# Bisection steps queued behind regular work, and duration estimates from measurements, in a hybrid encoder step

## The chip, the cores and the metric

The kernel runs on 1 core of one Trainium2 chip. The metric is device time in microseconds (us), the median of several runs: 1571.07 us before the change (3 runs, 1570.73 to 1572.39).

## The reference, cut to what matters

One layer of a streaming encoder runs on a prompt of 1024 frames (eight tiles of 128 rows) and on 8 samples of 16 new frames each with 512 cached keys (a ninth tile, called tile 8). Two mixers work side by side, a linear recurrence and a sparse attention, then a SwiGLU block. Everything is in float32.

```python
proj = rmsnorm(x, norm_mix) @ w_in                  # xr, gate, q, k, v, qi, ki, wi
xc = causal_conv(xr, conv_prev, conv_w, conv_b)     # 4 taps
r, i = sigmoid(xc @ w_rg + b_rg), sigmoid(xc @ w_ig + b_ig)     # 8 blocks of 64
h_t = a_t * h_(t-1) + sqrt(1 - a_t^2) * i_t * xc_t  # a = exp(-8 r softplus(-lambda))
y_a = h * gelu(gate)
idx = sum_h relu(qi_h . ki) * wi_h                  # indexer score per query and key
sel = top_k(where(chunk-causal, idx, -inf), 256)    # 132 for the samples
y_b = softmax(q . k[sel] / 8) @ v[sel]
x = x + concat(y_a, y_b) @ w_out
x = x + (silu(g) * u) @ w_ffn_out                   # g, u = rmsnorm(x) @ w_ffn_in
```

The top-k keeps for each query row the keys whose index score is among its best. The kernel doesn't sort: it finds each row's threshold by bisection and turns the scores into an additive mask.

## The kernel before, in words

Matrix products are done in float32 split into a high and a low part, so one product is three matmuls. The stages follow each other on TensorE: norm and key/value projection (to about 70 us), index scores (to 183), the recurrence, called LRU (to 355), query projection (to 433), first half of the output projection, called out-A, with rope of the keys (to 505), attention (to about 700), second half of the output projection, and the feed-forward block to the end.

**The bisection.** Tiles 2 to 8 need a threshold. Two groups are formed (TK): tiles 2 to 5 on ScalarE, where a count is a pass of Sign with an accumulator, and tiles 6, 7 and 8 on VectorE. VectorE's group copies the upper halves of the scores into 16-bit keys, does 16 rounds, makes new keys of the lower halves (topk_lower), does 16 more rounds, computes a threshold (topk_threshold) and turns each tile into a mask (topk_mask). A round is one count for each of the three tiles (tensor_scalar with accum_out, out to the scratch jk), and two to four operations on 128x3 numbers that set the next candidate. The masks of tile 6, 7 and 8 end in two GpSimd operations each. Attention on a tile waits for its mask; the samples wait for the masks of tile 7 and 8, because two constants of theirs are cast into the buffers of the keys and of the scratch.

**What sets the order.** Each stage is a set of Python generators, and run() steps them along a clock of its own. TensorE's time is added in mm(), that of the other engines in Metered.call, which raises busy[engine] by an estimate for each instruction. A generator yields how long its next step isn't due. The two bisections are "side" generators, tied to an engine by the table filler. Such a step is taken in run() when the clock has come to the engine's busy time less SLACKS[phase], and in fill() when a regular instruction leaves a gap of at least FILL = 1.0 us on its engine. All steps go through step(). The order in which instructions are handed out gives their priority; a scheduler behind it then orders each engine's queue by its own model of readiness and by priority. Before, step() lowers a bisection step's priority by 400 (LATER) and leaves the place to that scheduler.

On the chip each engine runs its queue in the order written; an instruction whose input isn't there holds what stands behind it.

Of the kernel before, what the change touches and what calls it, by code (L numbers as in the profile page):

```python
# [11 lines left out]
BF16 = mybir.dt.bfloat16  # L12
I32 = mybir.dt.int32
I16 = mybir.dt.int16
# [21 lines left out]
class Metered:  # L36


    def __init__(self, engine, kernel, name, fixed, each):
        self.engine, self.kernel, self.name, self.fixed, self.each = engine, kernel, name, fixed, each  # L40

    def __getattr__(self, op):
        f = getattr(self.engine, op)
        if op in ("dma_start", "wait", "semaphore") or not callable(f):
            return f

        def call(*args, **kw):
            n = 1
            for a in args:
                if hasattr(a, "shape") and len(a.shape) > 1:  # L50
                    n = max(n, int(np.prod(a.shape[1:])))
            each = self.each
            if self.name == "vector" and op in ("tensor_copy", "tensor_scalar") and "accum_out" not in kw:
                each *= 0.5
            if self.name == "vector" and kw.get("accum_out") is not None and args[1].dtype in (BF16, I16):
                each *= 0.5
            k = self.kernel
            start = k.now() if k.chain is None else k.chain + k.HOP
            k.fill(self.name, start)
            end = max(k.busy[self.name], start) + self.fixed + n * each  # L60
            if self.name == "scalar" and op == "activation":
                end += k.table(args[2])
            k.busy[self.name] = end
            if k.chain is not None:
                k.chain = end
            return f(*args, **kw)  # L66

        return call


class Engines:
    def __init__(self, nc, kernel):
        self.nc = nc
        for name, fixed, each in (("vector", 0.07, 0.00104), ("scalar", 0.2, 0.00072), ("gpsimd", 0.05, 0.0012)):
            kernel.busy[name] = 0.0
            setattr(self, name, Metered(getattr(nc, name), kernel, name, fixed, each))

    def __getattr__(self, x):
        return getattr(self.nc, x)
# [2 lines left out]
class Kernel:  # L82
    def __init__(self, ctx, tc, I, O):
        self.ctx, self.tc, self.I, self.O = ctx, tc, I, O
        self.pe = self.pe0 = 0.0
        self.clock = 0.0
        self.phase = 0
        self.chain = None
        self.busy, self.filler, self.side, self.gap = {}, {}, [], None
        self.nc = Engines(tc.nc, self)  # L90


    def run(self, streams, width, side=(), carry=()):
# [7 lines left out]
        def due(x):  # L101
            e = self.filler.get(x[1])
            return x[0] if e is None else max(x[0], self.busy[e] - self.SLACKS[self.phase])

# [49 lines left out]

    def step(self, g):

        n = self.LATER.get(self.filler.get(g), 0)
        if not n:
            return next(g, None)
        with self.tc.high_priority(offset=-n):  # L160
            return next(g, None)

    def begin(self):

# [27 lines left out]
    TABLES = {"exp": (AF.Exp, AF.Tanh), "sqrt": (AF.Sqrt,), "gelu": (AF.Gelu_apprx_tanh, AF.Tanh), "silu": (AF.Silu,)}  # L192
    SYNC = 0.3
    HOP = 0.1
    SLACKS = (1.5, 1.5, -3.0, -3.0, 1.5)
    QUEUE = 8.0
    AHEAD = 2.0

# [1 line left out]
    def mm(self, out, lhsT, rhs, start, stop):  # L200
        n = 1
        for v in rhs.shape[1:]:
            n *= v
        self.pe += max(n, 256 if lhsT.shape[-1] > 64 else 128) / 2400.0
        self.nc.tensor.matmul(out, lhsT, rhs, start=start, stop=stop)  # L205

    def mm4(self, out, lhsT, rhs, start, stop):
# [1538 lines left out]
```

## Time and profile before

| | before |
|---|---|
| median of 3 runs | 1571.07 us |
| the profiled execution | 1569.72 us |
| its span, first to last instruction | 1567.9 us |
| TensorE busy | 1446.7 us (92%) |
| VectorE busy | 916.7 us (58%) |
| ScalarE busy | 626.2 us (40%) |
| GpSimd busy | 312.8 us (20%) |
| mean granted TensorE clock | 0.96 |

The profile cuts the span into 40 slices and gives each engine's busy share in tenths, and it follows the chain of work that ended last. VectorE stands at 9 tenths or more from the sixth to the thirteenth slice and between 1 and 4 in most of the later half, while TensorE stands at 9 from the fourteenth slice on, the last excepted. Shares over the whole span therefore hide which engine sets the pace where. PE is TensorE, PEld its weight loads, DVE VectorE, ACT ScalarE, POOL GpSimd and SP the queue that issues transfers.

### The profile page before, as it was taken

The numbers are of one execution on the slowest core, as the hardware profiler recorded it, in microseconds if no ns is written. First come the engines' busy times: TensorE is split into PE (matmuls) and PEld (weight loads), VectorE is DVE, ScalarE is ACT, GpSimd is POOL, SyncE is SP. The second block draws the span as 40 slices with busy tenths as digits, with TensorE's granted clock in tenths as the row PEclk, the third lists the DMA queues.
The fourth block names the chain that finished last, engine by engine and source line by source line (L and its number), as shares of the span: only waits on it lengthen the run. The fifth ranks groups of instructions, "written<-read, shape, count | busy, mean of one in ns | idle before, by whom it ended". The sixth has DMA issues, their size and how long they took to land.

```text
span 1567.9 us, 20857 instructions
## 1 busy us (share of the span) xinstructions
PE 1446.7 (92%) x7754; PEld 1322.8 (84%) x7754; DVE 916.7 (58%) x1957; ACT 626.2 (40%) x1481; POOL 312.8 (20%) x453
## 2 busy tenths in 40 slices
PE   6889887756888999999999999999999999999998
PEld 6777777746766788888999999999898989898987
DVE  7556899999999888768324233333324242424143
ACT  6457968875633978655302020202120212111110
POOL 4215225541986434400000000000000000000000
PEclk8999898877898999999999999999999999999999
DMA  7201101100320002121202020202020201111003
GB/s 239 56 16 42 35 16 29 29 27 14 134 71 22 1 14 57 39 68 42 81 13 81 1 81 0 81 0 81 1 81 15 67 28 54 41 41 54 28 1 121
DMA packets 93797, 74.65 MB, mean 48 GB/s; under 512 B 13236, under 2 KB 84532, under 8 KB 93696
## 3 DMA queue, kind: packets, MB, share of 16 engines
q1 hardware_dynamic: 93696, 73.32, 15.5%
q8 instruction: 61, 1.00, 0.3%
q14 instruction: 40, 0.33, 0.1%
HBM read 67.03 MB, written 6.27 MB: 47 GB/s over the span
## 4 chain that ended last, share of the span: by engine, by line
PE 72%; DVE 18%; ACT 4%; issue 3%; DMA 1%; POOL 1%; SPq 0%; POOLq 0%; ACTq 0%; DVEq 0%
PE ps L205 67%; DVE jk L66 7%; PE ps L215 4%; DVE tk_cand L66 2%; DVE tr L66 1%; DVE xc L66 1%; ACT jk L66 1%; DVE qn L66 1%; DVE ti L66 1%; PE ps L210 1%; DVE tk_cnt L66 1%; DVE s L66 1%; DVE kn L66 0%; ACT relu L66 0%; DVE acc L66 0%
## 5 line engine op out<-in xcount | busy, mean ns | idle before, releaser
L205 PE MATMUL ps<-hf,w 128*128 128x384 f32 x2556 | 460.6, 338 | 0.0
L205 PEld LDWEIGHTS ps<-hf,w 128*128 128x128 f32 x2556 | 451.5, 187 | 0.8
L205 PE MATMUL ps<-w,a 128*128 128x512 f32 x999 | 239.1, 390 | 0.0
L66 DVE TENSOR_TENSOR acc<-ps,acc 128x512 f32<-128x512 f32 x234 | 161.3, 690 | 119.7 <-PE ps L205 119.2
L205 PEld LDWEIGHTS ps<-w,a 128*128 128x128 f32 x999 | 187.3, 188 | 40.1
L66 DVE TENSOR_TENSOR sg<-ps,sg 128x384 f32<-128x384 f32 x66 | 36.8, 557 | 281.7 <-PE ps L205 281.1
L66 ACT ACTIVATE w<-raw 128x512 fp32r<-128x512 f32 x128 | 77.7, 629 | 300.9 <-PE ps L205 220.0
L66 DVE TENSOR_TENSOR w<-raw,w 128x512 fp32r<-128x512 f32 x116 | 76.8, 688 | 85.0 <-ACT w L66 84.9
L66 ACT ACTIVATE a<-sg 128x384 fp32r<-128x384 f32 x66 | 34.5, 523 | 222.1 <-DVE sg L66 222.1
L66 ACT ACTIVATE jk<-s,tk_cand 128x384 bf16<-128x384 f32 (+3 forms) x128 | 99.8, 779 | 40.7 <-DVE tk_cand L66 36.8
L205 PE MATMUL ps<-hf,rest 128*128 128x384 f32 x612 | 114.5, 334 | 0.0
L205 PE MATMUL ps<-w,h 128*128 128x256 f32 (+1 forms) x600 | 102.6, 332 | 11.6 <-ACT sq L66 7.8
L205 PE MATMUL ps<-h,w 128*128 128x384 f32 x576 | 108.5, 348 | 0.5 <-ACT relu L66 0.5
L205 PEld LDWEIGHTS ps<-h,w 128*128 128x128 f32 x576 | 106.6, 198 | 0.6 <-ACT relu L66 0.6
L205 PEld LDWEIGHTS ps<-hf,rest 128*128 128x128 f32 x612 | 106.9, 188 | 0.2
L205 PEld LDWEIGHTS ps<-w,h 128*128 128x128 f32 x600 | 90.1, 207 | 18.3 <-ACT sq L66 8.2
L205 PE MATMUL ps<-w,rest 128*128 128x512 f32 x324 | 83.2, 406 | 11.3 <-POOL rest L66 11.1
L205 PEld LDWEIGHTS ps<-w,rest 128*128 128x128 f32 x324 | 61.0, 193 | 26.3 <-POOL rest L66 12.7
L66 ACT ACTIVATE sg<-ps 128x384 f32<-128x384 f32 x66 | 32.0, 485 | 121.3 <-PE ps L205 121.3
L205 PE MATMUL ps<-xh,bd 128*128 128x384 f32 x72 | 22.0, 426 | 46.3 <-ACT xh L66 40.6
L66 POOL TENSOR_SCALAR m<-m,mx 128x128 f32<-128x128 f32 (+7 forms) x64 | 47.5, 748 | 67.4 <-DVE mx L66 60.3
L205 PEld LDWEIGHTS ps<-xh,bd 128*128 128x128 f32 x72 | 15.1, 234 | 51.0 <-ACT xh L66 43.0
(263 smaller groups left out, 2221.0 us busy)
## 6 DMA issues: line engine op xcount, KB each, us to landing
raw<-in_w_ffn_in_dram SPq DMA_DIRECT2D x44, 512.0 KB, 3.9
raw<-in_w_ffn_out_dram SPq DMA_DIRECT2D x22, 512.0 KB, 3.6
raw<-in_w_in_dram SPq DMA_DIRECT2D x16, 512.0 KB, 5.1
out_dram<-acc SPq DMA_DIRECT2D x9, 512.0 KB, 2.6
x<-in_x_prompt_dram SPq DMA_DIRECT2D x8, 512.0 KB
acc<-in_x_prompt_dram SPq DMA_DIRECT2D x8, 512.0 KB, 4.2
tab<-in_rope_dram SPq DMA_DIRECT2D x34, 64.0 KB, 1.9
raw<-in_w_out_dram SPq DMA_DIRECT2D x4, 512.0 KB, 3.5
```

Of the source, the lines that this page charges most:

```text
L66: return f(*args, **kw)
L205: self.nc.tensor.matmul(out, lhsT, rhs, start=start, stop=stop)
L210: self.nc.tensor.matmul(out, lhsT, rhs, start=start, stop=stop)
L215: self.nc.tensor.transpose(out, in_, self.ident[0:n, 0:n])
```

## The change

Three things are changed. The estimates of VectorE, ScalarE and GpSimd are computed by a new function cost() with a fixed part and a part per element for each kind of operation; that of a matmul becomes its columns at 2.4 GHz plus 0.0167 us in place of at least 256 (or 128) columns. SLACKS becomes 0.5 in each phase. And each regular instruction of the three engines is recorded with its estimated end, so that step() can look up the last one on the step's engine whose end isn't later than the clock and give the step's instructions an edge to it: on that engine they may not stand ahead of it.

```diff
@@ -36,8 +36,8 @@
 class Metered:
 
 
-    def __init__(self, engine, kernel, name, fixed, each):
-        self.engine, self.kernel, self.name, self.fixed, self.each = engine, kernel, name, fixed, each
+    def __init__(self, engine, kernel, name):
+        self.engine, self.kernel, self.name = engine, kernel, name
 
     def __getattr__(self, op):
         f = getattr(self.engine, op)
@@ -45,35 +45,47 @@
             return f
 
         def call(*args, **kw):
-            n = 1
-            for a in args:
-                if hasattr(a, "shape") and len(a.shape) > 1:
-                    n = max(n, int(np.prod(a.shape[1:])))
-            each = self.each
-            if self.name == "vector" and op in ("tensor_copy", "tensor_scalar") and "accum_out" not in kw:
-                each *= 0.5
-            if self.name == "vector" and kw.get("accum_out") is not None and args[1].dtype in (BF16, I16):
-                each *= 0.5
             k = self.kernel
             start = k.now() if k.chain is None else k.chain + k.HOP
             k.fill(self.name, start)
-            end = max(k.busy[self.name], start) + self.fixed + n * each
+            end = max(k.busy[self.name], start) + self.cost(op, args, kw)
             if self.name == "scalar" and op == "activation":
                 end += k.table(args[2])
             k.busy[self.name] = end
             if k.chain is not None:
                 k.chain = end
-            return f(*args, **kw)
+            said = f(*args, **kw)
+            if not k.filling:
+                k.issued[self.name].append((end, said.ins))
+            return said
 
         return call
+
+    def cost(self, op, args, kw):
+        tensors = [a for a in args if hasattr(a, "shape") and len(a.shape) > 1]
+        n = max([1] + [int(np.prod(a.shape[1:])) for a in tensors])
+        wide = [a for a in tensors if int(np.prod(a.shape[1:])) == n]
+        here = all(a.space == bass.MemoryType.SB for a in wide)
+        accum = kw.get("accum_out") is not None or op == "tensor_tensor_reduce"
+        one = op in ("tensor_copy", "tensor_scalar", "memset")
+        if self.name == "scalar":
+            return 0.2 + n * 0.0008 + 0.19 * accum
+        if self.name == "gpsimd":
+            return 0.1 + n * 0.0011 if one else 0.2 + n * 0.0023
+        if op == "tensor_tensor_scan":
+            return 0.2 + n * 0.0022
+        if one and not accum:
+            return 0.1 + n * (0.00026 if here and all(a.dtype in (BF16, I16) for a in wide) else 0.00052 if here else 0.00104)
+        return 0.157 + n * 0.00104 + 0.08 * accum + 0.1 * (here and not one)
 
 
 class Engines:
     def __init__(self, nc, kernel):
         self.nc = nc
-        for name, fixed, each in (("vector", 0.07, 0.00104), ("scalar", 0.2, 0.00072), ("gpsimd", 0.05, 0.0012)):
+        for name in ("vector", "scalar", "gpsimd"):
             kernel.busy[name] = 0.0
-            setattr(self, name, Metered(getattr(nc, name), kernel, name, fixed, each))
+            kernel.issued[name] = []
+            setattr(self, name, Metered(getattr(nc, name), kernel, name))
 
     def __getattr__(self, x):
         return getattr(self.nc, x)
@@ -87,6 +99,7 @@
         self.phase = 0
         self.chain = None
         self.busy, self.filler, self.side, self.gap = {}, {}, [], None
+        self.issued, self.filling = {}, False
         self.nc = Engines(tc.nc, self)
 
 
@@ -154,11 +167,20 @@
 
     def step(self, g):
 
-        n = self.LATER.get(self.filler.get(g), 0)
-        if not n:
+
+        e = self.filler.get(g)
+        if e is None:
             return next(g, None)
-        with self.tc.high_priority(offset=-n):
-            return next(g, None)
+        now = self.clock if self.gap is None else self.gap
+        last = next((i for t, i in reversed(self.issued[e]) if t <= now), None)
+        with ExitStack() as st:
+            st.enter_context(self.tc.high_priority(offset=-self.LATER[e]))
+            if last is not None:
+                st.enter_context(self.tc.issue_after(last))
+            self.filling = True
+            lat = next(g, None)
+            self.filling = False
+        return lat
 
     def begin(self):
 
@@ -192,7 +214,7 @@
     TABLES = {"exp": (AF.Exp, AF.Tanh), "sqrt": (AF.Sqrt,), "gelu": (AF.Gelu_apprx_tanh, AF.Tanh), "silu": (AF.Silu,)}
     SYNC = 0.3
     HOP = 0.1
-    SLACKS = (1.5, 1.5, -3.0, -3.0, 1.5)
+    SLACKS = (0.5, 0.5, 0.5, 0.5, 0.5)
     QUEUE = 8.0
     AHEAD = 2.0
 
@@ -201,7 +223,7 @@
         n = 1
         for v in rhs.shape[1:]:
             n *= v
-        self.pe += max(n, 256 if lhsT.shape[-1] > 64 else 128) / 2400.0
+        self.pe += n / 2400.0 + 0.0167
         self.nc.tensor.matmul(out, lhsT, rhs, start=start, stop=stop)
 
     def mm4(self, out, lhsT, rhs, start, stop):
```

All instructions are the same ones and the same number of each; the last 4310 of TensorE's 7724 instructions stand in the same order. Three places where the order differs are shown. s_892, s_893 and s_894 are the scores of tiles 6, 7 and 8, s_889 to s_891 those of tiles 3 to 5; jk_911 is the scratch of VectorE's bisection, jk_912 of ScalarE's; sp_p, sp_e, prm and hb are small parameters of the recurrence, xc its convolution.

VectorE at the start of its bisection, before: the last index scores of tile 7 are followed by this.

```order
L66 SCALAR_TENSOR_TENSOR s_893<-relu,wi,s_893 128x512 x3
L66 MEMSET s_893 64x64
L66 COPY prm<-ps 128x160
L66 MEMSET sp_p 128x4
L66 COPY key<-s_893 128x1024
L66 TENSOR_SCALAR hb<-prm 128x8
L66 TENSOR_SCALAR sp_e<-prm 128x4
L66 TENSOR_SCALAR jk_911,tk_cnt<-key,tk_cand 128x1024
L66 TENSOR_TENSOR sp_e<-sp_e,prm 128x4
L66 TENSOR_SCALAR jk_911,tk_cnt<-key,tk_cand 128x528
```

Seven more counts stand between these rows and the first row of the convolution; some ten rows earlier tile 6's keys had been copied and counted, among tile 7's scores.

The same place in the changed order, up to the convolution.

```order
L57 TENSOR_TENSOR sp_p<-sp_p,sp_z 128x4
L57 TENSOR_SCALAR sp_p<-sp_p 128x4
L57 TENSOR_TENSOR sp_p<-sp_p,sp_s 128x4
L57 SCALAR_TENSOR_TENSOR sp_p<-sp_p,sp_e 128x4
L57 TENSOR_SCALAR sp_2069<-sp_p 128x4
L57 TENSOR_SCALAR m_2070<-sp_p 128x4
L57 TENSOR_SCALAR jk_911,tk_cnt<-key,tk_cand 128x896
L57 TENSOR_SCALAR jk_911,tk_cnt<-key,tk_cand 128x1024
L57 SCALAR_TENSOR_TENSOR xc<-xp,prm,xc 128x384
L57 TENSOR_SCALAR jk_911,tk_cnt<-key,tk_cand 128x528
L57 SCALAR_TENSOR_TENSOR xc<-xp,prm,xc 128x384
```

The three key copies stand ahead of these rows, among the steps of sp_p, and behind all index scores; two counts in place of ten stand ahead of the first convolution row.

VectorE at the end of its bisection, before: in out-A, among the rope of queries and keys, the last of tile 8.

```order
L66 TENSOR_TENSOR tail<-tail 128x72
L66 TENSOR_TENSOR qn<-qn,tab 128x256
L66 TENSOR_TENSOR kn<-kn,rp 128x128
L66 TENSOR_SCALAR jk_912,tk_cnt<-s_890,tk_cnt 128x640
L66 TENSOR_TENSOR acc<-ps,acc 128x512
L66 TENSOR_TENSOR qn<-qn,rp 128x256
L66 TENSOR_SCALAR tail<-tail 128x72
L66 TENSOR_TENSOR qn<-qn,rp 128x256
L66 CAST jk_911<-s_894 128x528
L66 TENSOR_SCALAR jk_912,tk_cnt<-s_891,tk_cnt 128x768
```

The cast of tile 8's finished scores stands long before attention begins.

The end of the bisection in the changed order: in attention; m<-ps,s_892 (named ISA) takes the masked scores of tile 6, and smr and rest are the split probabilities of tiles before it.

```order
L57 SCALAR_TENSOR_TENSOR key<-jk_911 128x896
L57 TENSOR_SCALAR s_892,tk_cnt<-s_892,tk_cnt 128x896
L57 TENSOR_TENSOR smr<-ps,smr 128x512
L57 TENSOR_SCALAR tk_cnt<-tk_cnt 128x1
L57 SCALAR_TENSOR_TENSOR jk_911<-key,tk_cnt,jk_911 128x896
L57 TENSOR_TENSOR smr<-ps,smr 128x512 x2
L57 TENSOR_SCALAR jk_911<-s_893,tk_cnt 128x1024
L57 SCALAR_TENSOR_TENSOR key<-jk_911 128x1024
L57 TENSOR_SCALAR s_893,tk_cnt<-s_893,tk_cnt 128x1024
L57 ISA m,mx<-ps,s_892 128x448
```

Ahead of attention's first row stood 96 counts and all masks before; now 72 counts stand there, and 24 counts and the masks of tiles 6, 7 and 8 come in attention.

TensorE at the first sample's scores (ps<-jk_911,key), before.

```order
L205 MATMUL ps<-k_4345,qeo 128x384
L205 MATMUL ps<-k_4346,qeo 128x384
L205 MATMUL ps<-k_4345,qeo 128x384
L205 MATMUL ps<-k_4346,qeo 128x384
L205 LDWEIGHTS key
L205 MATMUL ps<-jk_911,key 128x264
L205 MATMUL ps<-smr,rest 128x264
L215 MATMUL ps<-ident,m 128x128 x2
L205 LDWEIGHTS key
L205 MATMUL ps<-jk_911,key 128x264
```

They stand among the products of tile 5 (128x384), ahead of tile 6.

The same place in the changed order.

```order
L227 MATMUL ps<-k_4254,qeo 128x448
L227 MATMUL ps<-k_4253,qeo 128x448
L237 MATMUL ps<-ident,m 128x128
L227 MATMUL ps<-smr,vhl 128x512 x3
L237 MATMUL ps<-ident,m 128x128 x8
L227 MATMUL ps<-smr,vhl 128x512 x8
L227 LDWEIGHTS key
L227 MATMUL ps<-jk_911,key 128x264
L227 MATMUL ps<-rest 128x264 x3
L227 LDWEIGHTS key
```

They stand behind tile 6's first eight score products (128x448) and the last probability products of tile 5.

## Rows read from the trace of the kernel before

**Rows 1.** Five windows; columns: stretch, length, busy us per engine, granted clock, DMA share, GB/s.
```profile
core 0: us, PE busy (x) PEld busy (x) DVE busy (x) ACT busy (x) POOL busy (x), PEclk, DMA share, GB/s
0.00:174.00 174.00, 146.43 (x749) 123.38 (x749) 114.50 (x239) 104.77 (x262) 63.01 (x120) 0.92 0.29 84
174.00:200.00 26.00, 25.52 (x135) 23.33 (x135) 22.61 (x59) 25.29 (x54) 3.77 (x6) 1.00 0.09 23
200.00:507.00 307.00, 227.87 (x1233) 209.78 (x1232) 301.75 (x684) 189.78 (x519) 176.20 (x233) 0.86 0.14 44
507.00:585.00 78.00, 72.60 (x412) 61.43 (x412) 68.72 (x235) 66.44 (x162) 32.13 (x50) 0.94 0.03 8
585.00:1567.90 982.90, 974.24 (x5231) 904.92 (x5229) 409.09 (x746) 239.89 (x487) 37.67 (x44) 1.00 0.15 46
```

**Rows 2.** Groups of TensorE, 174 to 507 us: busy, mean ns, idle before, releaser.
```profile
L205 PE MATMUL ps<-xh,bd 128*128 128x384 f32 x72 | 22.0, 426 | 46.3 <-ACT xh L66 40.6 <-POOL xh L66 4.5 <-POOL xp L66 1.1
L205 PE MATMUL ps<-w,h 128*128 128x256 f32 x432 | 59.9, 305 | 11.6 <-ACT sq L66 7.8 <-DVE to L66 3.8
L205 PE MATMUL ps<-w,rest 128*128 128x512 f32 x108 | 31.1, 428 | 11.1 <-POOL rest L66 11.1
```

**Rows 3.** Groups of VectorE by shape, 200 to 507 us: counts of the bisection.
```profile
L66 DVE TENSOR_SCALAR_CACHE_REDUCE jk<-key,tk_cnt 128x1024 bf16<-128x1024 int16 x16 | 20.4, 1273 | 0.2
L66 DVE TENSOR_SCALAR_CACHE_REDUCE jk<-key,tk_cnt 128x896 bf16<-128x896 int16 x16 | 18.3, 1142 | 0.2
L66 DVE TENSOR_SCALAR_CACHE_REDUCE jk<-key,tk_cnt 128x528 bf16<-128x528 int16 x16 | 12.1, 756 | 0.2
L66 DVE DVE_READ_ACCUMULATOR jk<-key,tk_cnt 128x1 f32 x48 | 3.9, 81 | 0.0
L66 DVE TENSOR_SCALAR tk_cand<-tk_cnt 128x3 f32<-128x3 f32 x16 | 4.1, 258 | 0.2
L66 DVE SCALAR_TENSOR_TENSOR tk_cnt<-tk_cand,tk_cnt 128x3 f32<-128x3 f32 x16 | 4.1, 256 | 0.2
```

**Rows 4.** Timeline of VectorE, 410 to 460 us: mask of tile 7, and a cast.
```profile
426.22 0.94 DVE L66 TENSOR_SCALAR jk<-s,tk_cnt 128x1024 bf16<-128x1024 f32 x1
427.20 3.27 DVE L66 TENSOR_TENSOR_SCAN key<-jk 128x1024 int16<-128x1024 bf16 x1
430.39 1.25 DVE L66 TENSOR_SCALAR_CACHE_REDUCE s<-s,tk_cnt 128x1024 f32<-128x1024 f32 x1
433.13 1.27 DVE L66 SCALAR_TENSOR_TENSOR jk<-key,tk_cnt,jk 128x1024 bf16<-128x1024 int16 x1
435.40 2.64 DVE L66 CAST key<-ident 128x1024 bf16<-128x1024 f32 x1
```

**Rows 5.** Timeline of GpSimd, 440 to 460 us: last two mask steps of tile 8.
```profile
449.36 1.19 POOL L66 TENSOR_TENSOR s<-s,jk 128x528 f32<-128x528 f32 x1
451.96 0.84 POOL L66 TENSOR_SCALAR s<-s 128x528 f32<-128x528 f32 x1
```

**Rows 6.** Groups of VectorE by shape, 507 to 700 us: attention.
```profile
L66 DVE CUSTOM_DVE_ANT_0 m<-ps,s 128x448 f32<-128x448 f32 x8 | 5.0, 620 | 0.2
L66 DVE TENSOR_TENSOR smr<-ps,smr 128x512 fp32r<-128x512 f32 x60 | 40.6, 686 | 6.4 <-ACT smr L66 5.9
```

**Rows 7.** Timeline of TensorE, 570 to 592 us: first sample score, first product of tile 6.
```profile
575.34 0.27 PE L205 MATMUL ps<-jk,key 128*128 128x264 bf16 x1
583.20 0.98 PE L205 MATMUL ps<-k,qeo 128*128 128x448 f32 x4
```

**Rows 8.** Timeline of TensorE, VectorE and ScalarE around 205 us, a row or two each.
```profile
183.61 25.23 PE L205 MATMUL ps<-h,w 128*128 128x384 f32 x144 [0.48 <-ACT relu L66]
...
205.56 0.61 DVE L66 SCALAR_TENSOR_TENSOR xc<-xp,prm,xc 128x384 f32<-128x384 f32 x1
...
203.92 0.47 ACT L66 ACTIVATE xp<-ps 128x384 f32<-128x384 f32 x1
204.29 0.66 ACT L66 ACTIVATE xc<-ps,prm 128x384 f32<-128x384 f32 x1
```

**Rows 9.** Three more windows, columns as in the first group.
```profile
174.00:189.00 15.00, 14.52 (x72) 12.33 (x72) 13.22 (x27) 14.51 (x35) 0.31 (x1) 1.00 0.02 4
189.00:205.60 16.60, 16.60 (x98) 16.60 (x97) 14.98 (x59) 13.16 (x26) 3.66 (x6) 1.00 0.12 33
505.00:530.00 25.00, 20.20 (x102) 17.02 (x102) 22.30 (x88) 23.19 (x66) 9.01 (x21) 0.80 0.00 1
```

## The prediction

> **What bounds the kernel now.** I read the windows by stage first, then the groups of TensorE and VectorE in the stretch where neither is full, then the timelines at the places the change moves. From 585 us on TensorE is busy 974.24 of 982.9 us at a granted clock of 1.00 [rows 1]. Its last 4310 instructions keep their order, so this stretch can't gain more than its 8.7 idle us; what the change does before it shifts its start. Ahead of it the other engine is full: from 200 to 507 us VectorE is busy 301.75 of 307 us, 98.3%, and TensorE only 227.87, at a clock of 0.86 [rows 1]. TensorE's waits there look like the loss: 46.3 us ahead of the gate products of the recurrence, 40.6 of them until ScalarE's xh, which stands behind VectorE's convolution; 11.6 ahead of the query projection and 11.1 in out-A, the last until GpSimd [rows 2]. But a VectorE that is never idle sets the pace whatever its order. What the reader is to see in these rows is that TensorE's waits there are paid back only if VectorE's work leaves the stretch for a place where it is idle. Between 507 and 585 us, in attention, it is idle for 78 - 68.72 = 9.3 us [rows 1]. That is all the room there is.
>
> **What the change moves.** Nothing is added or removed. 24 of the 96 counts, that is eight rounds, and the three masks go from ahead of attention into it. A round costs 1273 + 1142 + 756 ns of counts, 3 x 81 for reading the accumulators, 258 and 256 for the two small operations [rows 3]: 3.93 us, eight of them 31.4. The mask of tile 7 costs 0.94 + 3.27 + 1.25 + 1.27 = 6.73 us [rows 4]; by width (896 + 1024 + 528 over 1024) the three together cost 16.1, and the cast of the keys 2.64 [rows 4]. Some 50 us of VectorE's work leave the recurrence, the query projection and out-A, so attention will begin earlier, by up to 50 us, with fewer waits for xh. But they land on a stretch that has 9.3 us free, and tile 6 and the samples wait for the end of them. The 78 us between attention's start and tile 6 become about 68.72 + 50 = 119. So the sum is best made at the point where TensorE needs the bisection's end, which is the first sample's score: there all of VectorE's work has to be done in either order.
>
> **First term, the work up to there.** By 585 us VectorE has been busy 114.50 + 22.61 + 301.75 + 68.72 = 507.6 us [rows 1] and idle 77.4. In the changed order the same work stands ahead of the sample's score, and beside it four reductions of tile 6 (about 0.65 us each) and three splits (0.69) [rows 6] with three reciprocals, less the five small operations of the first sample that had come sooner: about 3.5 us more. The last cast then waits for GpSimd's two operations on tile 8, 1.19 + 0.84 = 2.0 us [rows 5]. With 77.4 us idle as before that is 590.5 us. Before, the first sample's score came at 575.34 and tile 6's first product at 583.20 [rows 7]; 33 instructions of 0.1 to 0.2 us, that follow this product in the changed order and here alike, put the equal point at about 588. So +2.5 us.
>
> **Second term, a later start.** Before, ten counts stand ahead of the first convolution, at 205.56 us [rows 8]; now two. Eight counts with their small operations, about 10 us by the prices above, leave a stretch in which VectorE is busy 13.22 of 15.0 and 14.98 of 16.6 us [rows 9], because the keys now wait behind all index scores and a chain of small operations on the recurrence's parameters. They come later instead, but the convolution can't fill the hole at once. TensorE's run of 144 products takes 25.23 us from 183.61 [rows 8]; the first product that it needs is done after 96 of them, at 200.4, and ScalarE adds 0.47 + 0.66 [rows 8]: 201.6 at the earliest, 4 us sooner than now. 10 - 4 = 6 us of new idle time. The bounds are 0, if index scoring itself ends sooner, and 10, if the convolution comes no sooner. I take 6.
>
> **Third term, idle time after it.** Before, VectorE is idle 5.25 us from 200 to 507 (1.7%) and 9.3 from 507 to 585 (11.9%) [rows 1]. A step that queues behind regular work also waits when that work is late, and the planner counts TensorE at full clock while 0.86 was granted [rows 1], so regular work will be later than planned. On the other side there is now work to fill attention's holes. The trace doesn't show such a wait. From below it costs nothing and the holes close to 1% of the 386 us from 200 us to the first sample's score: 4 us, 10.6 less than the 14.5 of now. From above the rate of attention now holds everywhere: 11.9% of 386, 46 us, 31 more. I take 3% of the 267 us up to attention (8.0), nearest to the row from 200 to 507, and 7% of attention's 119 (8.3), between the two rows: 16.3, so +1.8.
>
> **Fourth term, the restart.** While the masks are made TensorE runs out of work; a first score has to pass VectorE, ScalarE and GpSimd before it is transposed. At attention's start now, where the same happens, TensorE is busy 20.20 of 25 us at a granted clock of 0.80 [rows 9]: 4.8 us idle, and 5 lost to the lower of its two levels. Here more streams are under way, so I take a quarter of these 10, 2.5; the bounds are 0 and 10.
>
> **The sum.** 2.5 + 6 + 1.8 + 2.5 = +12.8 us on the profiled execution's 1569.7 (its span of 1567.9 and 1.8 around it): 1582.5. That execution lies 1.4 us under the median of the runs, so the forecast is 1584 us, slower by 0.8%. Where this is right, the own range of this case is 1575 to 1594.
>
> **A rule to weigh.** The rows above say that moving VectorE's work out of a full stretch pays only as far as another stretch has room, 9.3 us [rows 1]. The Trainium skill (Perfetto Trace Analysis, Optimization Strategy) says that where the most-contended engine changes over time, performance may be improved by interleaving the regimes. Here VectorE is full to 507 us and TensorE from 585 on [rows 1], so by this rule the change goes in the right direction, and the time would fall. By my sum it doesn't, since the dependence of tile 6 and the samples on the masks keeps the moved work out of the regime of TensorE.
>
> **Rivals.** *Faster: the holes close.* The regular work is planned well, VectorE starts its bisection as early as now and is idle for 1% alone. Then 2.5 + 0 - 10.6 + 0 = -8, which gives 1563. For it speaks that both ends are bounds that nothing excludes, and that the moved steps are short (about 1 us) beside the holes; against it, that the keys visibly stand behind more work than before. It decides the matter if VectorE's idle time up to the first sample's score stays under 75 us. *No change: the same work in another order.* The later start is paid back by fewer holes in attention (+6 and -9) and the rest cancels: 1571. For it speaks that VectorE's work is the same and nearly all of it is on the path; against it the restart. *Much slower: the edge holds VectorE.* Steps wait behind regular work that is late by the planner's optimism, and the idle rate is 6 to 12% throughout: 23 to 46 us in place of 14.5, with the other terms 2.5 + 6 + 2.5 to 10, which gives 1591 to 1621, about 1605. For it speaks the clock of 0.86; against it, that VectorE is the late one nearly everywhere, and a late engine finds its inputs ready. That the change doesn't do what it says is excluded by the order: the counts have moved.
>
> **Chances.** The forecast 0.43, faster 0.24, no change 0.17, much slower 0.16. A measurement of this kernel tells 0.2%, about 3 us, from no change. Faster is then 0.24, the same 0.17, slower 0.43 + 0.16 = 0.59. The range reaches from just under the faster case, 1561, to the middle of the slowest, 1606.
>
> **What would show it.** In the profile after: the first key copy not at 174 but behind the last index score, near 190 to 198 us; TensorE's wait for xh well under 40.6 us and the stretch to attention's first row shorter by 20 to 40 us; counts in attention and VectorE over 93% busy there; TensorE nearly idle for 10 to 20 us ahead of the first sample's score, and this score at 585 to 605 us; from there to the end 975 to 985 us as now. It would be wrong if the first sample's score came before 580, or if TensorE found other work while the masks are made.

## The result, and the profile after

The changed kernel takes 1617.8 us (median of 4 runs, 1613.76 to 1619.98) against 1570.9 for the kernel before (4 runs, 1569.27 to 1572.39): a ratio of 1.0296, with a 95% interval of 1.0273 to 1.0319. It is slower, as forecast, but by 46.9 us in place of 13, and outside the range. By its time the case that came true is the one given 0.16, an edge that holds VectorE (1591 to 1621 us); the reason given for it holds only in part, as the runs below show. The profiled execution took 1618.24 us for a span of 1616.3.

The first view is the windows of the changed kernel, cut at the same events as [rows 1]: the start of attention's first row is now at 491.7 us (507 before), the first sample's score at 620.9.

```profile
core 0: us, PE busy (x) PEld busy (x) DVE busy (x) ACT busy (x) POOL busy (x), PEclk, DMA share, GB/s
0.00:174.00 174.00, 147.06 (x749) 124.40 (x750) 115.94 (x235) 98.59 (x243) 64.72 (x120) 0.92 0.29 84
174.00:200.00 26.00, 26.00 (x132) 23.32 (x131) 17.66 (x58) 24.00 (x51) 1.53 (x4) 0.96 0.09 23
200.00:491.70 291.70, 226.28 (x1234) 210.25 (x1232) 262.00 (x596) 196.39 (x537) 162.78 (x229) 0.89 0.15 45
491.70:620.90 129.20, 90.69 (x436) 71.42 (x435) 116.00 (x333) 73.08 (x169) 44.19 (x58) 0.80 0.02 7
620.90:1616.30 995.40, 979.95 (x5211) 909.40 (x5210) 406.79 (x737) 236.51 (x483) 35.50 (x42) 0.99 0.15 46
```

The kernel before, cut once at the prediction's equal point, 588 us.

```profile
0.00:588.00 588.00, 475.43 (x2543) 420.54 (x2544) 510.21 (x1221) 388.15 (x998) 275.97 (x411) 0.90 0.17 50
588.00:1567.90 979.90, 971.24 (x5213) 902.30 (x5211) 406.46 (x737) 238.02 (x484) 36.81 (x44) 1.00 0.15 46
```

The loss has two parts: 620.9 - 588 = 32.9 us up to the sample's score, and 995.4 - 979.9 = 15.5 after it, together the 48.4 by which the span grew (1567.9 to 1616.3). Up to that point VectorE did the same work, 115.94 + 17.66 + 262.00 + 116.00 = 511.6 us against 510.2. What grew is its idle time: 620.9 - 511.6 = 109.3 us against 588 - 510.2 = 77.8. From 200 us to attention it is idle for 29.7 us, where [rows 1] has 5.25 up to 507 us. Who released it there, by the list of waits of VectorE from 202 to 491.7 us:

```profile
DVE tt L57 <- ACT tr L57: 6.8, 4, 2.1
DVE ti L57 <- ACT tr L57: 3.8, 3, 1.6
DVE ti L57 <- ACT ti L57: 3.6, 3, 2.4
DVE tk_cand L57 <- ACT jk L57: 3.2, 4, 1.5
DVE xc L57 <- ACT xc L57: 2.4, 2, 1.8
DVE qn L57 <- POOL rp L57: 1.9, 1, 1.9
```

Columns: total us, times, longest. For the most part VectorE stands at regular instructions of the recurrence (tt, ti, xc) whose inputs ScalarE has not made; the row of tk_cand is a step of ScalarE's own bisection that VectorE does for it, and qn waits for GpSimd. One such place, in VectorE's timeline:

```profile
314.69 1.27 DVE L57 TENSOR_SCALAR_CACHE_REDUCE jk<-key,tk_cand 128x1024 bf16<-128x1024 bf16 x1
...
316.07 0.17 DVE L57 TENSOR_SCALAR tk_cand<-tk_cand 128x4 int32<-128x4 int32 x1
318.66 0.56 DVE L57 SCALAR_TENSOR_TENSOR ti<-ti,xc 128x384 f32<-128x384 f32 x1 [2.42 <-ACT ti L57]
321.01 1.27 DVE L57 SCALAR_TENSOR_TENSOR xc<-xp,prm,xc 128x384 f32<-128x384 f32 x2 [1.79 <-ACT xc L57]
...
342.25 0.75 DVE L57 TENSOR_SCALAR_CACHE_REDUCE jk<-key,tk_cand 128x528 bf16<-128x528 bf16 x1
```

The last row is tile 8's count of the round that the first row belongs to. It needs only VectorE's tk_cand of that round, which was there before 314 us, and would have taken 0.75 us of the first hole of 2.42, and the next round's steps could have followed; but it stands 26 us behind. At the end of the bisection TensorE runs dry:

```profile
600.95 2.22 PE L227 MATMUL ps<-smr,vhl 128*128 128x512 f32 x5 [0.34 <-DVE smr L57]
620.86 0.38 PE L227 MATMUL ps<-jk,key 128*128 128x264 bf16 x1 [17.68 <-DVE jk L57]
```

Before, the same score came at 575.34 without a wait [rows 7].

### The profile page after: what moved, and what is told of

It reads as the page before. It is cut to its first block, busy times and chain, and to the rows that moved or that the text cites. A ratio compares the mean times of both kernels' runs of the same rounds, so it can differ in the third digit from the quotient of the medians.

```text
span 1616.3 us, 20863 instructions
## 1 busy us (share of the span) xinstructions
PE 1470.0 (91%) x7754; PEld 1338.8 (83%) x7754; DVE 918.4 (57%) x1957; ACT 628.6 (39%) x1481; POOL 308.7 (19%) x453
## 4 chain that ended last, share of the span: by engine, by line
PE 67%; DVE 18%; ACT 6%; issue 5%; POOL 2%; DMA 1%; SPq 0%; POOLq 0%; DVEq 0%; ACTq 0%
PE ps L227 63%; DVE jk L57 5%; PE ps L237 3%; DVE tk_cand L57 2%; ACT jk L57 2%; DVE qn L57 1%; DVE m L57 1%; DVE tr L57 1%; DVE xc L57 1%; DVE ti L57 1%; PE ps L232 1%; DVE s L57 1%; ACT L57 1%; DVE acc L57 1%; POOL s L57 1%
## 5 line engine op out<-in xcount | busy, mean ns | idle before, releaser
L227 PE MATMUL ps<-h,w 128*128 128x384 f32 x576 | 113.9, 359 | 0.0
L227 PEld LDWEIGHTS ps<-h,w 128*128 128x128 f32 x576 | 111.5, 206 | 0.0
L227 PE MATMUL ps<-w,h 128*128 128x256 f32 (+1 forms) x600 | 98.8, 324 | 4.0 <-ACT sq L57 2.5
L227 PEld LDWEIGHTS ps<-w,h 128*128 128x128 f32 x600 | 87.3, 199 | 11.1 <-ACT sq L57 3.2
L227 PE MATMUL ps<-smr,vhl 128*128 128x512 f32 x165 | 59.9, 447 | 10.0 <-ACT smr L57 7.3
L57 ACT ACTIVATE m<-m,mx 128x128 f32<-128x128 f32 (+7 forms) x64 | 49.4, 773 | 37.8 <-DVE mx L57 34.0
L57 POOL TENSOR_SCALAR m<-m,mx 128x128 f32<-128x128 f32 (+7 forms) x64 | 47.7, 754 | 84.5 <-DVE mx L57 68.8
## 6 DMA issues: line engine op xcount, KB each, us to landing
raw<-in_w_ffn_in_dram SPq DMA_DIRECT2D x44, 512.0 KB, 3.8
raw<-in_w_ffn_out_dram SPq DMA_DIRECT2D x22, 512.0 KB, 3.5
raw<-in_w_in_dram SPq DMA_DIRECT2D x16, 512.0 KB, 3.9
out_dram<-acc SPq DMA_DIRECT2D x9, 512.0 KB, 2.8
x<-in_x_prompt_dram SPq DMA_DIRECT2D x8, 512.0 KB
acc<-in_x_prompt_dram SPq DMA_DIRECT2D x8, 512.0 KB
raw<-in_w_out_dram SPq DMA_DIRECT2D x4, 512.0 KB, 3.6
```

The source lines that it names most:

```text
L57: said = f(*args, **kw)
```

## The experiments

Sixteen kernels were run. The edits to the changed kernel are shown against it, the others against the kernel before. "Point" is the later of the first sample's score and tile 6's first score product; work and idle time are VectorE's from 0 to it; "ahead" counts VectorE's 96 counts that stand ahead of attention's first row.

| kernel | us | ahead | point | work | idle |
|---|---|---|---|---|---|
| before | 1571 | 96 | 583.2 | 505.8 | 77.4 |
| e2 edge only | 1575.5 | 96 | 589.9 | 505.4 | 84.5 |
| e7 SLACKS only | 1576.0 | 96 | 590.2 | 501.2 | 89.0 |
| e8 matmul count only | 1577.5 | 96 | 592.4 | 502.2 | 90.3 |
| e6 all estimates only | 1582.6 | 96 | 594.1 | 508.1 | 86.0 |
| e12 slower TensorE | 1580.5 | 96 | 592.0 | 505.8 | 86.3 |
| e3 edge and SLACKS | 1590.0 | 96 | 603.1 | 503.3 | 99.7 |
| e1 estimates and SLACKS, no edge | 1591.7 | 96 | 602.3 | 512.0 | 90.3 |
| e9 all, counts at half | 1593.7 | 96 | 602.1 | 506.4 | 95.7 |
| e5 all, edge up to attention | 1601.9 | 96 | 607.7 | 506.7 | 101.0 |
| e10 all, edge 120 us back | 1605.1 | 87 | 611.9 | 511.3 | 100.6 |
| e11 estimates and edge | 1610.2 | 79 | 619.4 | 511.3 | 108.1 |
| e4 all, edge in attention alone | 1618.2 | 72 | 620.8 | 509.3 | 111.5 |
| changed kernel | 1617.8 | 72 | 620.9 | 511.6 | 109.3 |
| e13 changed, samples first | 1612.3 | 72 | 630.6 | 513.3 | 117.3 |
| e14 e1, samples first | 1587.1 | 96 | 604.5 | 516.2 | 88.4 |
| e15 before, samples first | 1574.7 | 96 | 594.9 | 511.2 | 83.7 |
| e16 before, tile 6 first | 1590.0 | 96 | 597.3 | 515.7 | 81.7 |

VectorE's work is 501 to 516 us in all of them; in the rows down to the changed kernel, which keep attention's order of handing out, its idle time goes from 77.4 to 111.5 us, and the time follows it for the most part: the time less the idle time is 1487 to 1502 us in nine of them, and 1501 to 1509 in e1, e4, e5, e10 and the changed kernel, to which the last group of experiments comes back.

**e1, no edge.**

```diff
-            if last is not None:
+            if last is not None and False:
```

> New estimates and SLACKS, but no edge: the scheduler may pull bisection steps forward again. In this order all 96 counts stand ahead of attention's first row (9 ahead of the first convolution). Theory A (the loss is the work that the edge keeps back until attention, so that TensorE starves ahead of the first sample's score): 1568 to 1582 us, VectorE idle 200 to 507 us near 5, first sample's score at 575 to 590. Theory B (the edge makes VectorE and ScalarE stand at late regular work, wherever the counts are): the same time, since no edge is left. Theory C (the new estimates and SLACKS make the order of the regular work worse, the edge is innocent): 1600 us or more.

1591.66 us, ratio 1.0138 (1.0123 to 1.0153). None of the theories A, B and C: without the edge 21 us of the loss stay, 26 go. So the edge is more than half of it, and estimates and SLACKS cost something of themselves, which I had not put a price on.

**e2, the edge alone.** The kernel before with the recording of issued instructions and step() as changed; estimates, SLACKS and matmul count as before.

```diff
+            if last is not None:
+                st.enter_context(self.tc.issue_after(last))
```

> The kernel before with the edge alone: old estimates, old SLACKS, old count of a matmul. In this order the 96 counts still stand ahead of attention (7 ahead of the first convolution, 60 ahead of its last row, where before has 10 and 65). Theory A: 1568 to 1582 us, since hardly anything moves into attention. Theory B: VectorE idle 15 to 35 us between 200 and 507 us, and 1585 to 1605 us. Theory C: as before, 1568 to 1574.

1575.45 us, 1.0033 (1.0020 to 1.0046). An edge by itself costs 5 us, with VectorE idle for 7 us more, most of it ahead of 200 us, since the first key copy waits until 192.64 us (174.34 before). Theory B's 15 to 35 us of idle time from 200 to 507 us don't come (6.6 did): with the old estimates and SLACKS the edge holds VectorE little.

**e4 and e5, the edge in attention and up to it.**

```diff
# e4
+            if last is not None and self.phase >= 4:
# e5
+            if last is not None and self.phase < 4:
```

> The changed kernel with the edge only for steps handed out in attention. Up to the last convolution VectorE's order is that of the kernel without an edge (66 counts there), and 72 counts stand ahead of attention, as in the changed kernel. Theory A: most of the loss is there, 1595 to 1618 us, with TensorE idle 10 to 20 us ahead of the first sample's score. Theory B: the waits in the recurrence are gone, and with them 20 to 30 us: 1580 to 1595. Theory C: 1600 or more.

> The other half: the edge for steps handed out up to attention, none in it. VectorE has the changed kernel's order in the recurrence (2 counts ahead of the first convolution, 44 ahead of its last row), but all 96 counts stand ahead of attention. Theory A: 1570 to 1585 us. Theory B: VectorE idle about 30 us between 200 and 507 us as in the changed kernel, 1595 to 1610. Theory C: 1600 or more.

e4: 1618.24 us, 1.0299 (1.0282 to 1.0316), as much as the changed kernel. e5: 1601.92, 1.0195 (1.0177 to 1.0213). The edge on steps handed out in attention alone costs 26.6 us more than none (e1); the whole edge costs 26.1, and the edge up to attention alone 10.3, so the two halves don't add. Where the 26.6 are lost is seen in the windows of e1 and of e4, whose orders are alike up to the last convolution. First e1:

```profile
200.00:300.00 100.00, 67.83 (x332) 65.39 (x331) 97.34 (x259) 73.69 (x147) 37.32 (x58) 0.83 0.08 23
300.00:507.00 207.00, 162.43 (x909) 147.57 (x908) 200.49 (x413) 116.00 (x366) 135.71 (x175) 0.89 0.17 53
```

Then e4:

```profile
200.00:300.00 100.00, 68.00 (x332) 65.58 (x331) 97.35 (x258) 73.61 (x146) 37.29 (x57) 0.83 0.09 23
300.00:507.00 207.00, 167.58 (x941) 152.54 (x940) 172.63 (x389) 128.13 (x403) 127.08 (x182) 0.88 0.16 53
```

They agree to 300 us. From 300 to 507 VectorE is busy for 200.5 us in e1 and 172.6 in e4: 27.9 us more of holes. The balance up to each point, cut at attention's first row, e1 and then e4:

```profile
200.00:514.75 314.75, 234.18 (x1252) 216.02 (x1250) 305.13 (x690) 196.44 (x528) 175.60 (x235) 0.86 0.14 42
514.75:602.27 87.52, 75.80 (x419) 65.07 (x419) 70.65 (x236) 67.41 (x158) 32.51 (x50) 0.90 0.04 10
```

```profile
200.00:494.79 294.79, 228.85 (x1246) 212.61 (x1244) 259.09 (x599) 193.74 (x523) 160.63 (x229) 0.88 0.14 45
494.79:620.81 126.02, 86.51 (x434) 68.79 (x434) 114.07 (x332) 73.38 (x169) 45.62 (x58) 0.84 0.02 7
```

Ahead of attention VectorE is idle for 9.6 us in e1 and 35.7 in e4, in attention for 16.9 and 12.0: 21.2 us more in all, with 2.7 us less work, and the point comes 18.5 us later. The rest of the loss, 4.9 of the 23.4 us between these two profiled executions, comes behind the point. It is the place of the loss that surprised me: not in attention, where the edge acts, but ahead of it. VectorE's timeline at 390 us, in e1:

```profile
389.48 1.27 DVE L57 TENSOR_SCALAR_CACHE_REDUCE jk<-key,tk_cnt 128x1024 bf16<-128x1024 int16 x1
...
390.79 0.76 DVE L57 TENSOR_SCALAR_CACHE_REDUCE jk<-key,tk_cnt 128x528 bf16<-128x528 int16 x1
...
396.58 0.25 DVE L57 RECIPROCAL nr<-nr 128x18 f32<-128x18 f32 x1
...
413.19 0.75 DVE L57 TENSOR_SCALAR_CACHE_REDUCE jk<-key,tk_cnt 128x528 bf16<-128x528 int16 x1
```

and in e4:

```profile
389.22 0.27 DVE L57 RECIPROCAL nr<-nr 128x18 f32<-128x18 f32 x1 [3.71 <-ACT nr L57]
...
391.96 0.67 DVE L57 TENSOR_TENSOR qn<-qn,tab 128x256 f32<-128x256 f32 x1 [1.84 <-POOL rp L57]
...
407.62 0.53 DVE L57 TENSOR_TENSOR qn<-qn,tab 128x256 f32<-128x256 f32 x1 [2.01 <-POOL rp L57]
...
495.00 1.14 DVE L57 TENSOR_SCALAR_CACHE_REDUCE jk<-key,tk_cnt 128x896 bf16<-128x896 int16 x1
```

Both have done 72 counts by 368 us. In e1 the other 24, which the planner handed out only in attention, follow at once, pulled forward by the scheduler behind it; the last is the row at 413.19, and the wait for nr is covered. In e4 the edge keeps them in attention, from 495.00 to 588 us, and the holes ahead of it stay empty. ScalarE's bisection, which the edge binds too, isn't what it delays here: its last count starts at 424.38 us in e4 and at 442.62 in e1. e5 has its idle time in the recurrence, as the changed kernel does (27.7 us from 200 us to attention), but all 96 counts ahead of attention, and costs 10 us more than e1, in theory B's range: theory A holds for most of the edge, theory B for this part.

**e6, e7, e8, e3: the parts alone, and the edge without the estimates.** e6 has the new cost() and the new count in mm(); e3 is the changed kernel with the old estimates of both.

```diff
# e6 and e8, in mm(); e6 has the new cost() too
-        self.pe += max(n, 256 if lhsT.shape[-1] > 64 else 128) / 2400.0
+        self.pe += n / 2400.0 + 0.0167
# e7
-    SLACKS = (1.5, 1.5, -3.0, -3.0, 1.5)
+    SLACKS = (0.5, 0.5, 0.5, 0.5, 0.5)
# e3, against the changed kernel: cost() gives what the old Metered.call added
-        self.pe += n / 2400.0 + 0.0167
+        self.pe += max(n, 256 if lhsT.shape[-1] > 64 else 128) / 2400.0
```

> The kernel before with the new estimates alone (the engines' costs and the count of a matmul): old SLACKS, no edge. The run without an edge lost 21.6 us although all its counts stood ahead of attention, so estimates and SLACKS cost something of themselves. Theory C1 (the estimates make the order of the regular work worse): 1585 to 1595 us. Theory C2 (the SLACKS do, by handing out steps of the bisection at other times): 1568 to 1576 us.

> The kernel before with SLACKS of 0.5 in all phases, old estimates, no edge. Theory C1: 1568 to 1576 us. Theory C2: 1583 to 1593 us. ScalarE's last step of the bisection stands behind attention's first rows here (some 55 VectorE rows later), which by either theory costs a few us at attention's start at most.

> The kernel before with the new count of a matmul alone, so that the planner takes TensorE to be faster; old costs of the engines, old SLACKS, no edge. If the loss of the estimates lies in TensorE's count (the granted clock of 0.86 makes TensorE slower than the planner then thinks): 1583 to 1595 us. If it lies in the engines' costs: 1568 to 1576 us. By theory C2 also 1568 to 1576.

> The changed kernel (edge, SLACKS 0.5) with the old estimates for engines and matmuls. All 96 counts stand ahead of attention's first row in this order. Theory A and C1 (the estimates first delay the handing out, and the edge then keeps it so): 1570 to 1582 us. Theory B (the edge makes the engines stand): 1590 to 1605. Theory C2: 1590 to 1600, the loss of the SLACKS with the edge's 5 us.

Measured 1582.58 (ratio 1.0078, 1.0063 to 1.0093), 1576.00 (1.0029, 1.0018 to 1.0040), 1577.48 (1.0042, 1.0027 to 1.0057) and 1590.00 (1.0122, 1.0107 to 1.0137). Against 1571.0 the estimates cost 11.5 us, 6.4 of them by the count of a matmul alone, the SLACKS 5.0 and the edge 5.4 (e2). That adds up to 22; the three together cost 47. Edge and SLACKS (e3) cost 19, more than their 10.4, and e3's price came out as theory B or C2 had it, not as A. Neither C1 nor C2 is right alone. With all 96 counts ahead of attention the edge thus costs 5.4 us (e2), 10.3 (e5 against e1) or 14.0 (e3 against e7), so not all of its price is moved counts. Where e3 and e7 lose their time shows in the stretch from the last count's end to attention's first row, in the kernel before, e7 and e3:

```profile
408.40:507.00 98.60, 76.27 (x365) 63.47 (x363) 95.95 (x182) 39.23 (x177) 83.26 (x101) 0.89 0.23 76
```

```profile
413.00:507.80 94.80, 74.05 (x348) 61.57 (x347) 83.05 (x169) 37.55 (x169) 73.69 (x98) 0.88 0.21 71
```

```profile
416.60:519.50 102.90, 73.15 (x325) 60.16 (x324) 83.23 (x178) 52.86 (x194) 61.54 (x84) 0.85 0.19 65
```

From 300 us to the last count VectorE is idle for 1 to 2 us in each; behind it, where no count is left to cover a wait, for 2.7 us before, 11.8 in e7 and 19.7 in e3. In e3 VectorE also waits longer for ScalarE, whose last count starts at 495.53 us (429.65 in e7). How the estimates cost their 11.5 us was not followed further.

**e9, the counts' estimate taken back; e10, an edge 120 us back; e11, the old SLACKS.**

```diff
# e9, in cost()
+        if accum and args[1].dtype in (BF16, I16):
+            return 0.07 + n * 0.00052
# e10, in step()
+        last = next((i for t, i in reversed(self.issued[e]) if t <= now - 120.0), None)
# e11
+    SLACKS = (1.5, 1.5, -3.0, -3.0, 1.5)
```

> The changed kernel (edge everywhere, SLACKS 0.5, new estimates) with one estimate taken back: a count of the bisection costs 0.07 us and 0.00052 us per element, 0.60 us for 1024 columns where the trace shows 1.27. By the order all 96 counts stand ahead of attention's first row (55 ahead of the last convolution row; 72 and 44 in the changed kernel). Theory H (the true, longer estimate of a count makes the planner hand out 24 counts only in attention, and the edge keeps them there, so that holes of VectorE before attention stay empty): the 26 us of the edge in attention go, 1588 to 1600 us, VectorE idle 300 to 507 us under 15. Theory B (the edge makes the engines stand, whatever is handed out when): 1608 to 1620.

> The changed kernel, but the edge goes to the last regular instruction that ends 120 us before the planner's clock, so that a step may be pulled forward by up to 120 us. 87 of the 96 counts stand ahead of attention (72 with the edge at the clock, 96 without an edge), 66 ahead of the last convolution row (44, 66). Theory H: between the two by the counts, 1591.7 + 9/24 of 26.6, about 1602 us, range 1595 to 1608. Theory B: an edge that far back holds nobody, 1590 to 1595.

> The changed kernel with the SLACKS of before: edge and new estimates together. 79 counts stand ahead of attention. Theory H: the estimates alone (1582.6) and 17/24 of the edge's 26.6 us, about 1601, range 1596 to 1608. If the three edits simply add: 11.5 for the estimates and 5 for the edge, 1587 us.

e9: 1593.65 us, 1.0149 (1.0134 to 1.0164). With one estimate made wrong again, 24 of the 47 us are gone, edge and all. The old formula counted 0.60 us for a count of 1024 columns, the new one 0.157 + 1.065 + 0.08 = 1.30, and the trace has 1.273 [rows 3]. With the true number the planner finds room for fewer rounds ahead of attention. With the edge this costs 24 us (1617.8 against 1593.65); without it all the new estimates together cost 11.5 (e6), and that of a count was not tried alone. VectorE is idle for 10.6 us from 300 to 507 us here, the columns as above:

```profile
300.00:507.00 207.00, 146.69 (x824) 132.89 (x823) 196.41 (x427) 112.79 (x365) 127.72 (x167) 0.85 0.16 53
```

e10: 1605.13, 1.0219 (1.0203 to 1.0236), between the two as theory H had it (1602), and not at theory B's 1590 to 1595. e11: 1610.16, 1.0254 (1.0239 to 1.0270): the three edits don't add (1587 expected then), but theory H's 1601 is 9 us short as well, for a reason that was not found; TensorE waits there for 22.5 us in one piece at the first sample's score:

```profile
PE ps L227 <- DVE jk L57: 22.5, 1, 22.5
```

**e12, a slower TensorE in the planner.**

```diff
-        self.pe += max(n, 256 if lhsT.shape[-1] > 64 else 128) / 2400.0
+        self.pe += max(n, 256 if lhsT.shape[-1] > 64 else 128) / 2200.0
```

> The kernel before with one edit: a matmul is counted at 2200 columns per us in place of 2400, so that the planner takes TensorE to be 9% slower, nearer to the granted clock of 0.86 between 200 and 507 us. The new count, which makes TensorE faster in the planner's eyes, alone cost 6.4 us. If that was the planner's distance from the true pace: a gain, 1562 to 1569 us. If any other order of the regular work than the one of before costs a few us: 1572 to 1580.

1580.54, 1.0067 (1.0050 to 1.0084). A planner nearer to the true pace is slower too, just above the second range. Each way of leaving the old numbers (e6, e7, e8, e12) cost 5 to 12 us, with 9 to 13 us more of VectorE's idle time; that is what shows, and not that either estimate is the better one.

**e13 to e16, tile 6 and the samples.** The 15.5 us that the changed kernel lost behind the first sample's score were still open. In the changed kernel and in e1, e4, e5 and e10 eight of tile 6's score products stand ahead of that score.

```diff
# e13, e14 and e15: ATT_ORDER
-... x in ((6 + b // 2, b % 2), ("s", 2 * b), ("s", 2 * b + 1))
+... x in (("s", 2 * b), ("s", 2 * b + 1), (6 + b // 2, b % 2))
# e16: both head pairs of tile 6 ahead of the first samples
+... + ((6, 0), (6, 1)) + tuple(x for b in range(4) for x in ((("s", 2 * b), ("s", 2 * b + 1)) if b < 2 else ((7, b % 2), ("s", 2 * b), ("s", 2 * b + 1))))
```

> The changed kernel with one edit: in attention's order each pair of samples is handed out ahead of the head pair of tile 6 or 7 that it followed. On TensorE none of tile 6's products stands ahead of the first sample's score then. Theory S (tile 6's products ahead of the samples cost some 11 us after that score): 1604 to 1610 us. Theory R (a late bisection and TensorE's restart cost them): 1614 to 1621.

> The same edit on the kernel with the new estimates and SLACKS and no edge (1591.7 us). Theory S: 1578 to 1584 us. Theory R: 1589 to 1595, as without the edit.

> The same edit on the kernel before, where no product of tile 6 stood ahead of the samples anyway. Both theories: 1568 to 1576 us, about the same; a gain of more than 3 us would make it the best kernel of the study.

> The opposite edit on the kernel before: both head pairs of tile 6 are handed out ahead of the first samples, so that 20 of tile 6's products stand ahead of the first sample's score. Theory S: 1579 to 1590 us. Theory R: 1568 to 1575, since the bisection ends as early as before.

1612.33 (ratio 1.0267, 1.0248 to 1.0286), 1587.12 (1.0101, 1.0086 to 1.0116), 1574.68 (1.0025, 1.0015 to 1.0034) and 1589.99 (1.0125, 1.0110 to 1.0140). Putting tile 6 ahead costs the kernel before 19 us, which speaks for theory S; putting the samples ahead gives the changed kernel and e1 only 5.5 and 4.5 us back, half of what S had and between the two ranges. So this order is at most about a third of the 15.5 us. No kernel of the study beats the one before.

## Why the prediction was wrong, by its own steps

**The point and the method were right.** The sum was made on VectorE's work and idle time up to the first sample's score, and there work and idle time do account for it. The first term put the work and GpSimd's last wait at 513.1 us (507.6 + 3.5 + 2.0); measured are 511.6 of work, and that wait:

```profile
617.57 0.77 DVE L57 SCALAR_TENSOR_TENSOR jk<-key,tk_cnt,jk 128x528 bf16<-128x528 int16 x1
620.37 0.43 DVE L57 CAST jk<-s 128x528 bf16<-128x528 f32 x1 [2.03 <-POOL s L57]
```

**The later start was nearly right.** The first key copy came at 195.80 us (forecast 190 to 198) and the first convolution row at 202.24 (201.6 at the earliest). VectorE's idle time up to 200 us grew from 62.9 to 174 + 26 - 115.94 - 17.66 = 66.4: 3.5 us where the second term had 6.

**The third term failed.** I gave VectorE 16.3 us of idle time from 200 us to the sample's score; it had 29.7 + 13.2 = 42.9, two of which the first term had already. That is 24.6 us of the 35.6 by which the sum fell short, and the score, forecast for 585 to 605 us, came at 620.9. I took 3% up to attention and 7% in it; it was 10.2% in both. The step in the text that failed is the argument against the rival: "that VectorE is the late one nearly everywhere, and a late engine finds its inputs ready". It holds for an engine whose holes something fills. Before, the bisection filled them: a count stood wherever a regular input was late, which made VectorE look like an engine that is never idle [rows 1]. I read its 98.3% as proof that it set the pace whatever the order; the 98.3% was the result of an order in which ready work stood beside late work. With the same instructions in other orders VectorE's share from 200 us to attention is 89.8% in the changed kernel (262.00 of 291.7 us) and 87.9% in e4 (259.09 of 294.79). The rival's own reason, regular work that is late by the planner's optimism, is only part of it: the edge costs 5 us in e2, and 10 and 14 in e5 and e3, where no count has moved into attention. e4, e9 and e1 show the larger part: a true estimate of the counts makes the planner hand 24 of them out in attention, and the edge forbids the scheduler to bring them back.

**The fourth term was too small.** 2.5 us were given to the restart, with 10 as the upper bound; 15.5 were lost after the score. All but 0.2 us of it lies between the score and the place where TensorE's last 4310 instructions begin, 790.90 us in the changed kernel:

```profile
620.90:790.90 170.00, 158.94 (x902) 137.52 (x901) 116.96 (x280) 96.90 (x224) 35.50 (x42) 0.93 0.17 47
790.90:1616.30 825.40, 821.00 (x4312) 771.88 (x4310) 289.82 (x459) 139.61 (x260) 0.00 (x0) 1.00 0.15 45
```

and 742.67 us before:

```profile
588.00:742.67 154.67, 150.43 (x904) 130.63 (x902) 116.36 (x279) 98.28 (x225) 36.81 (x44) 0.99 0.19 52
742.67:1567.90 825.23, 820.81 (x4311) 771.67 (x4310) 290.11 (x459) 139.75 (x261) 0.00 (x0) 1.00 0.15 45
```

The last 4310 take the same time, as the prediction had it. But it took them for the whole stretch from 585 us on ("from there to the end 975 to 985 us as now"); they begin only at 742.67, and ahead of that the order was free to change. There 154.67 us became 170.00. TensorE's idle time went from 4.2 to 11.1 us, 6.8 more, and its busy time for nearly the same number of matmuls from 150.4 to 158.9, 8.5 more, at a granted clock of 0.93 against 0.99. The clock was lowest, 0.69 from 620.90 to 630 us, right behind the wait of 17.7 us. So the term had its parts right, idle time and clock, and their size wrong. e13 takes 5.5 us off the whole kernel by the order of samples and tile 6; which streams cause the later idle time is not settled.

**The waits of TensorE.** xh was to wait for well under 40.6 us, and attention to begin 20 to 40 us sooner. It began 15.3 us sooner, and the wait stayed:

```profile
L227 PE MATMUL ps<-xh,bd 128*128 128x384 f32 x72 | 19.1, 383 | 41.0 <-ACT xh L57 40.7 <-POOL xh L57 0.3
```

In the other runs ScalarE's xh costs it between 34.7 us (e7, with 11 counts ahead of the first convolution row) and 46.4 (e1, with 9), and 38.9 in e9 with 2. Taking counts of VectorE out of its way doesn't shorten it, so their number doesn't set it; what does was not tried. VectorE was to be over 93% busy in attention and was 116.00 of 129.2, 90%. TensorE's dry stretch of 10 to 20 us ahead of the sample's score came, with 17.7.

**The rule on interleaving** that the prediction weighs (the Trainium skill, Perfetto Trace Analysis, Optimization Strategy) would have had the time fall. It rose, but the runs are no test of the rule: as the prediction said, the moved counts stayed ahead of the stretch where TensorE is full. In attention VectorE was busy for 116.00 of 129.2 us and TensorE for 90.69. What the runs show is a price for such a move: 24 counts moved into attention cost 26 us (e1 and e4), since they gate tile 6 and the samples and had covered holes where they were.

## What to carry to other kernels

A filler that can run anywhere is worth its place beside late work. An edge that pins it to a planner's clock takes that away, and here it was paid for where the holes were, 367 to 495 us in e4, ahead of the place where the edge holds the counts. So ask of an engine that is never idle what fills its holes, and whether the change lets it go on doing so. A planner's number that is nearer to the measured duration isn't a gain by itself: here the true price of a count, with the edge, moved 24 counts out of the stretch whose holes they had covered, and the old, wrong one kept them there.

## What the runs showed of the hardware

The cast into the buffer of the keys, 128x1024 from f32 to bf16, takes 2.64 us in the kernel before [rows 4] and 0.69 in the changed one. In the kernel before, GpSimd's timeline has an operation of two SBUF inputs that starts just before the cast, at 435.31 us, so that VectorE's row (435.40 to 438.04) seems to hold a wait for its end at 437.49:

```profile
435.31 2.18 POOL L66 TENSOR_TENSOR s<-s,jk 128x1024 f32<-128x1024 f32 x1
```

In the changed kernel VectorE's cast comes first, and GpSimd's row, of the same operation and size, is the longer one:

```profile
610.76 0.69 DVE L57 CAST key<-ident 128x1024 bf16<-128x1024 f32 x1
```

```profile
610.81 2.62 POOL L57 TENSOR_TENSOR s<-s,jk 128x1024 f32<-128x1024 f32 x1 [6.96 <-DVE mx L57]
```

The Trainium skill (SBUF — State Buffer, SBUF: two separate sides) says that GpSimd shares a pair of ports with those operations of VectorE that use both of its port pairs, or have two inputs in SBUF, and that the pair is an exclusive lock, which the one that starts first holds for the whole instruction. These rows, one place in each kernel, agree with it. By this reading VectorE's busy time holds some such waits, so that its 505.8 us of work before are not all work, and of the 2.64 us that the prediction moved for this cast some 2 were not the cast's own.
